# A hybrid scan and attention block on one core: attention, gate and scan interleaved by new costs, and the two maps combined off VectorE

## The chip, the cores and the metric

The kernel runs on one core of a Trainium2 chip. The metric is the device time of one execution in microseconds; the time of the kernel before is the median of three runs.

## The reference, cut to what matters

One layer of a backbone block: 1024 latent and 256 context tokens, width 1024. One input projection feeds two groups. One is a bidirectional Mamba-2 scan (16 heads of 64 in two groups of states, chunks of 128 tokens, forward and backward, with a SiLU gate `z`); the other is differential attention with 4 heads, two softmax maps each. Both outputs are normed, concatenated and projected; a gated MLP follows.

```python
def diff_attention(q, k, v, lam):
    s = jnp.einsum('bqhcd,bkhcd->bhcqk', q.astype(F32), k.astype(F32)) * (DA_QK_DIM ** -0.5)
    p = jax.nn.softmax(s, axis=-1)
    w = p[:, :, 0] - lam * p[:, :, 1]
    return jnp.einsum('bhqk,bkhe->bqhe', w, v.astype(F32))
...
    y_diag = jnp.einsum('bclsgr,bcsgrp->bclgrp', w, xs)
    y_off = jnp.einsum('bclgn,bcgrpn,bclgr->bclgrp', cm, h_starts, jnp.exp(a_cum))
    return y_diag + y_off
...
        yd = _ssd_finish(ssd_chunk_outputs(xs_l, dtl, b_l, c_l, acum_l, hs_l) + dsk * xs_l, rev)
        y_l = yd if y_l is None else y_l + yd
...
    ys_l = rmsnorm(ys_l.astype(pl.dtype) * jax.nn.silu(zl), ssd_norm_g)
```

## The kernel before

`build` runs the stages one after the other: `startup`, `inproj` (all of the input projection but the gate), then the stretch of this change, then `mixffn` (output projection and MLP). In the stretch PE alternates between attention and a filler.

`attention` is a generator over 32 steps n (4 heads x 8 tiles of 128 queries). A step computes two score maps of 128 x 1280 (`scores`, tile `sc`; L814 takes the maximum on VectorE, L815 the exponential on ScalarE into `et`), combines the two maps of the step before in `weigh` (L820 to L823), transposes the result in three pieces on PE (`transpose`, tile `tr`, copied to `wt`) and, for every second step, multiplies with the values (`values`, tile `po`; L851 copies to `oo`, which is stored to `od`). Heads 0 and 1 take 30 value products (split operands), heads 2 and 3 ten. `load_head` loads query tiles S, keys K and values V of a head when its first step comes.

The filler is first `zproj` (384 gate products, tile `pz`, in 16 tiles of 128 x 512; `zo`, the SiLU gate, is stored to `zt`), then `ssd`: states backward (`state`, tiles `xw`, `s`, `hb`), forward (`H0`), and for each of 8 chunks and two groups the function `go` (tiles `scs`, `G`, `yo`, `t`, `y`, `yg`), then `finish` (tile `yt`, gated with `zc` and stored to `yd`).

`run` interleaves them: each `yield` of attention gives a gap in us, times a fill factor; the filler is advanced until the costs that it yields have used up the gap. `self.pin` keeps PE's instructions in the order in which the code issues them; other engines follow the order that a scheduler gives. All loads and stores of the stretch go through SP's queue in the order in which they stand there. What is left of the scan after the last step is run by `ssd_rest` inside `mixffn`, together with the first parts of the attention norm: `o` is loaded from `od` (L1051), squared and summed over columns (`cs_ps`, `cr_ps`), the factor is spread (`dg`, `bc_ps`) and applied (L1062); `yl` is the scan's output loaded back from `yd` (L1072). `pw`, the first output product, follows.

## Time and profile before

| | us |
| --- | --- |
| median of three runs | 1826.5 (1822.24 to 1832.29) |
| the profiled execution | 1826.04 |
| its span | 1824.2 |
| first gate product (`pz`) to first output product (`pw`) | 417.2 to 889.2 |
| PE busy in the span | 1601.6 (88%) |
| VectorE / ScalarE / GpSimd busy | 1222.1 / 753.6 / 1081.2 |

The profile calls TensorE PE, VectorE DVE, ScalarE ACT, GpSimd POOL and the engine that issues the loads SP. A row of a timeline gives the start in us, the duration, the engine, the line, the operation, the tile written and those read, and in brackets how long the engine stood idle ahead of it and what released it. Every matmul but the transposes has the line of a helper, L145, so PE is read by tiles. Records of matmuls overlap, so the price of a packed product is the distance between starts.

### The profile page before, as it was taken

The numbers are of one execution on the slowest core, as the hardware profiler recorded it, in microseconds if no ns is written. First come the engines' busy times: TensorE is split into PE (matmuls) and PEld (weight loads), VectorE is DVE, ScalarE is ACT, GpSimd is POOL, SyncE is SP. The second block draws the span as 40 slices with busy tenths as digits, with TensorE's granted clock in tenths as the row PEclk, the third lists the DMA queues.
The fourth block names the chain that finished last, engine by engine and source line by source line (L and its number), as shares of the span: only waits on it lengthen the run. The fifth ranks groups of instructions, "written<-read, shape, count | busy, mean of one in ns | idle before, by whom it ended". The sixth has DMA issues, their size and how long they took to land.

```text
span 1824.2 us, 21276 instructions
## 1 busy us (share of the span) xinstructions
PE 1601.6 (88%) x7588; PEld 1266.8 (69%) x7588; DVE 1222.1 (67%) x1442; ACT 753.6 (41%) x1395; POOL 1081.2 (59%) x710
## 2 busy tenths in 40 slices
PE   6998998996999888888998958989989998989976
PEld 2797877784778655665677746767777776767755
DVE  4569633352656577877764588766667677898886
ACT  4533676631444333444443443333323334344242
POOL 3322678772100155658566767777778887778741
PEclk8999999998999899999999989999999998999997
DMA  8276767667131667447553312222222225744222
GB/s 310 96 241 218 239 217 246 242 215 224 56 104 46 197 218 213 127 143 234 179 166 114 107 47 98 87 87 93 98 87 87 100 99 187 252 156 127 67 75 93
DMA packets 138826, 273.35 MB, mean 150 GB/s; under 512 B 11984, under 2 KB 60544, under 8 KB 138208
## 3 DMA queue, kind: packets, MB, share of 16 engines
q1 hardware_dynamic: 138128, 271.03, 45.0%
q8 instruction: 60, 0.98, 0.2%
q0 software_dynamic: 592, 0.96, 0.2%
q14 instruction: 46, 0.38, 0.1%
HBM read 197.63 MB, written 74.32 MB: 149 GB/s over the span
## 4 chain that ended last, share of the span: by engine, by line
PE 39%; DVE 18%; POOL 17%; DMA 11%; issue 8%; ACT 6%; SPq 0%; POOLq 0%; DVEq 0%; ACTq 0%
PE pu L145 9%; POOL wlo L126 6%; PE pd L145 6%; POOL S L1205 4%; PE lat L145 4%; PE pz L145 3%; PE pb L145 3%; PE sc L145 3%; DMA K<-kd 3%; PE pw L145 2%; DVE T L126 2%; DMA wt<-wmB 2%; DMA gd<-R 2%; PE po L145 2%; DMA R<-atd 2%
## 5 line engine op out<-in xcount | busy, mean ns | idle before, releaser
L145 PE MATMUL pu<-T,whi 128*128 128x512 f32 x1232 | 387.8, 396 | 8.7 <-ACT whi L125 8.7
L145 PE MATMUL pu<-T,wlo 128*128 128x512 f32 x616 | 248.7, 404 | 44.5 <-POOL wlo L126 36.9
L145 PEld LDWEIGHTS pu<-T,whi 128*128 128x128 f32 x1232 | 235.8, 191 | 58.2 <-ACT whi L125 9.1
L126 POOL TENSOR_TENSOR wlo<-wraw,whi 128x512 fp32r<-128x512 f32 (+2 forms) x118 | 163.4, 1388 | 101.3 <-ACT whi L125 101.2
L145 PE MATMUL lat<-hl,w_hi 128*128 128x512 f32 x640 | 204.6, 396 | 3.0 <-DVE tm L685 2.1
L145 PE MATMUL pd<-T,whi 128*128 128x512 f32 x560 | 183.2, 408 | 15.1 <-ACT whi L125 7.5
L126 POOL TENSOR_TENSOR w_lo<-w_raw,w_hi 128x1024 fp32r<-128x1024 f32 (+1 forms) x36 | 82.7, 2299 | 178.7 <-ACT w_hi L125 156.9
L126 POOL TENSOR_TENSOR wlo<-S,whi 128x512 fp32r<-128x512 f32 (+2 forms) x122 | 171.0, 1411 | 27.6 <-ACT whi L125 27.6
L145 PEld LDWEIGHTS pu<-T,wlo 128*128 128x128 f32 x616 | 117.8, 191 | 86.2 <-POOL wlo L126 49.3
L814 DVE TENSOR_REDUCE stat<-sc 128x1 f32<-128x1280 f32 x64 | 95.2, 1488 | 104.2 <-PE sc L145 104.2
L125 ACT CAST whi<-wraw 128x512 fp32r<-128x512 f32 (+2 forms) x140 | 81.3, 583 | 196.8 <-PE pu L145 108.8
L125 ACT CAST whi<-S 128x512 fp32r<-128x512 f32 (+2 forms) x144 | 81.9, 573 | 150.0 <-PE pu L145 94.7
L145 PEld LDWEIGHTS lat<-hl,w_hi 128*128 128x128 f32 x640 | 121.8, 191 | 28.5 <-DVE tm L685 2.5
L145 PEld LDWEIGHTS pd<-T,whi 128*128 128x128 f32 x560 | 109.5, 197 | 44.2 <-DVE T L126 12.3
L815 ACT ACTIVATE et<-sc,stat 128x1280 f32<-128x1280 f32 x64 | 85.1, 1330 | 130.0 <-DVE stat L814 128.4
L145 PE MATMUL sc<-K,S 128*128 128x512 f32 (+1 forms) x384 | 97.5, 390 | 45.8 <-DMA K<-kd 24.1
L145 PE MATMUL pd<-T,wlo 128*128 128x512 f32 x280 | 115.3, 412 | 15.5 <-POOL wlo L126 15.3
L145 PE MATMUL lat<-hl,w_lo 128*128 128x512 f32 x320 | 126.8, 396 | 0.0
L145 PEld LDWEIGHTS sc<-K,S 128*128 128x128 f32 x384 | 73.5, 200 | 72.8 <-ACT et L815 30.1
L538 POOL TENSOR_TENSOR R<-R,never 128x1024 f32<-128x1024 f32 x32 | 80.6, 2533 | 43.1 <-DMA R<-atd 41.4
L542 ACT ACTIVATE R<-R,lna 128x128 f32<-128x128 f32 x256 | 78.3, 393 | 56.7 <-POOL R L538 56.6
L908 POOL TENSOR_TENSOR xw<-xt,dte 128x1024 f32<-128x1024 f32 x18 | 36.8, 2049 | 93.7 <-DMA xt<-xtok 71.4
(280 smaller groups left out, 3682.0 us busy)
## 6 DMA issues: line engine op xcount, KB each, us to landing
wraw<-wUp SPq DMA_DIRECT2D x46, 512.0 KB, 3.3
wt<-wmB SPq DMA_DIRECT2D x32, 512.0 KB, 4.5
R<-atd SPq DMA_DIRECT2D x32, 512.0 KB, 5.6
stg<-gf_d SPq DMA_DIRECT2D x21, 768.0 KB, 4.8
w_raw<-wU SPq DMA_DIRECT2D x28, 512.0 KB, 5.1
gf_d<-T SPq DMA_DIRECT2D x11, 1024.0 KB, 4.2
K<-kd SPq DMA_DIRECT2D x32, 320.0 KB, 7.8
xt<-xtok SPq DMA_DIRECT2D x19, 512.0 KB, 5.2
```

What stands on the lines that cost most here:

```text
L125: nc.scalar.copy(hi, src)
L126: (lo_eng or nc.vector).tensor_tensor(out=lo, in0=src, in1=hi, op=ALU.subtract)
L145: self.pe(self.nc.tensor.matmul(out, lhsT=lhsT, rhs=rhs, start=start, stop=stop))
L538: nc.gpsimd.tensor_tensor(out=R[:, d], in0=R[:, d], in1=self.never[:, d].unsqueeze(1).broadcast_to([P, 8, P]), op=ALU.add)
L542: nc.scalar.activation(e, e, AF.Exp, bias=self.lna[:, d, i, h:h + 1], scale=1.0)
L814: nc.vector.tensor_reduce(out=st[:, c:c + 1], in_=sc, axis=AX.X, op=ALU.max, negate=True)
L815: nc.scalar.activation(et, sc, AF.Exp, bias=st[:, c:c + 1], accum_out=acc)
L908: nc.gpsimd.tensor_tensor(out=h3(xw), in0=h3(xt), in1=bc_h(self.dte, d, i), op=ALU.mult)
L1205: nc.gpsimd.tensor_tensor(out=t, in0=in0, in1=in1, op=op)
```

## The change

All of it lies between `inproj` and `mixffn`. One balance `self.debt` is carried from the gate products to the scan, with one factor `FILL`; the gaps are new (`FIRST_GAP`, `HEAD_GAP`, `G_ONE`, `G_VAL`, `G_TWO`), and so are the filler's costs. Head 1's keys are loaded into the same pool at step 8 with a gap behind them, and its values at step 10. Head 2 gets a pool of its own, `ap2`, and is loaded when `ssd` starts; head 3 is loaded at step 18. In `weigh` the combination of the maps, one VectorE instruction, becomes a product on ScalarE and a sum on GpSimd. The third transposed piece of heads 2 and 3 is copied by ScalarE.

In the scan the skip term `dsum * x * gate` is computed beside the gate (`zx`, from `xct`, which `inproj` now stores) and added at the end by GpSimd; the chunk's products with `ea` and their sum are made by VectorE straight from PSUM, and `G` is multiplied from PSUM without ScalarE's copy. The state's decay on GpSimd is issued in two halves. `et` has four buffers instead of three, `wt` three instead of four, V one instead of two.

```diff
 F32_FROM = 2
-WT_ENG = "aad"
+WT_ENG = "aaa"
...
-G_B = 2.3
+S_COST = 1.75
+Z_COST = 0.69
+G_ONE = 3.6
+G_VAL = 0.2, 0.2, 1.2, 1.2
+G_TWO = 1.0, 1.0, 0.8
+HEAD_GAP = 4.0
...
 E_W = "ggv"
-FIRST_GAP = 12.0
+FIRST_GAP = 27.0
...
 Y_STEPS = 0, 1, 2, 3, 4, 5, 6, 7, 8, 11, 14
-B_FILL = 1.1
+FILL = 0.98
...
 
-    def run(self, at, filler, fill, drain):
-
-        debt = 0.0
-        for tile_no, gap in at:
-            debt += fill * gap
-            while debt > 0:
+    def run(self, at, filler, drain):
+
+        while True:
+            while self.debt > 0:
                 cost = next(filler, None)
                 if cost is None:
                     if not drain:
                         return
                     break
-                debt -= cost
+                self.debt -= cost
+            gap = next(at, None)
+            if gap is None:
+                return
+            self.debt += FILL * gap
...
-                    if u >= U_B:
+                    if u < U_B:
+                        nc.sync.dma_start(self.xct[u], y[:, CTX:])
+                    else:
                         g = (u - U_B) % 2
                         nc.sync.dma_start((self.bt if u < U_C else self.ct)[g], y[:, CTX:])
...
                              k == 0, k == KT - 1)
                     if k < KT - 1:
-                        yield 0.65
-                zo = zp.tile([P, 512], F32, name="zo")
+                        yield Z_COST
+                xc = zp.tile([P, 512], F32, name="xc", bufs=1)
+                nc.sync.dma_start(xc, self.xct[u][:, sl])
+                zo = zp.tile([P, 512], F32, name="zo", bufs=4)
                 nc.scalar.activation(zo, p, AF.Tanh, scale=0.5)
                 nc.vector.scalar_tensor_tensor(out=zo, in0=zo, scalar=1.0, in1=p, op0=ALU.add, op1=ALU.mult)
                 nc.sync.dma_start(self.zt[u][:, sl], zo)
-                yield 0.65
+                nc.vector.scalar_tensor_tensor(out=xc, in0=xc, scalar=self.dsum[:, u:u + 1], in1=zo,
+                                               op0=ALU.mult, op1=ALU.mult)
+                nc.sync.dma_start(self.zx[u][:, sl], xc)
+                yield Z_COST
...
-            v = []
+            return S, K, []
+
+        def load_values(h, ap):
             for s in range(1 if h >= F32_FROM else 2):
-                vt = ap.tile([P, NT, VD], F32R, name=f"V{s}")
+                vt = ap.tile([P, NT, VD], F32R, name=f"V{s}", bufs=1)
                 nc.sync.dma_start(r32(vt), r32(self.vd[h, s]))
-                v.append(vt)
-            return S, K, v
+                heads[h][2].append(vt)
...
                     self.mm(sc[:, o:o + w], S[c][:, qt * P:(qt + 1) * P], K[c][i][:, o:o + w], i == 0, i == 1)
-            et = ap.tile([P, TOK], F32, name="et", bufs=3)
+            et = ap.tile([P, TOK], F32, name="et", bufs=4)
...
             nc.vector.reciprocal(out=st[:, 5:6], in_=st[:, 4:5])
-            nc.vector.scalar_tensor_tensor(out=st[:, 6:7], in0=st[:, 5:6], scalar=self.nlam[:, 0:1],
-                                           in1=self.s0[:, qt, h:h + 1], op0=ALU.mult, op1=ALU.mult)
-            nc.vector.scalar_tensor_tensor(out=ex[0], in0=ex[1], scalar=st[:, 6:7], in1=ex[0], op0=ALU.mult, op1=ALU.add)
+            nc.vector.tensor_scalar(out=st[:, 6:7], in0=st[:, 5:6], scalar1=self.nlam[:, 0:1],
+                                    scalar2=self.s0[:, qt, h:h + 1], op0=ALU.mult, op1=ALU.mult)
+            nc.scalar.mul(ex[1], ex[1], st[:, 6:7])
+            nc.gpsimd.tensor_tensor(out=ex[0], in0=ex[0], in1=ex[1], op=ALU.add)
...
+        def prefetch(h, pool=ap):
+            heads[h] = load_head(h, pool)
+            if h != 1:
+                load_values(h, pool)
+
+        self.prefetch = prefetch
         n_all = DA_H * NL
         wt, done, prev = None, None, None
         for n in range(n_all + 2):
+            if n in (0, NL, 2 * NL + 2):
+                prefetch({0: 0, NL: 1, 2 * NL + 2: 3}[n])
+                yield {0: FIRST_GAP, NL: HEAD_GAP}.get(n, 0.0)
+            if n == NL + 2:
+                load_values(1, ap)
             if n < n_all:
-                if n % NL == 0:
-                    heads[n // NL] = load_head(n // NL)
-                if n == 0:
-                    yield n, FIRST_GAP
                 st = ap.tile([P, 8], F32, name="stat", bufs=4)
                 e0 = scores(n, 0, st)
             if done is not None:
                 values(*done)
+                yield G_VAL[done[0] // NL]
                 done = None
-                long = False
-            else:
-                long = True
-                yield n, G_LONG if n < n_all else 2.0
+            elif n < n_all:
+                yield G_ONE
             if prev is not None:
                 m, pst, pex = prev
                 w = weigh(m, pst, pex)
             if n < n_all:
                 e1 = scores(n, 1, st)
+            yield G_TWO[0]
             if prev is not None:
                 if m % 2 == 0:
-                    wt = [[ap.tile([P, 4, 256], F32R, name=f"wt{s}", bufs=4) for s in range(2)] for _ in range(3)]
+                    wt = [[ap.tile([P, 4, 256], F32R, name=f"wt{s}", bufs=3) for s in range(2)] for _ in range(3)]
                 for gi in range(2):
                     transpose(m, w, wt, gi)
-                yield n, G_A if long else G_B
+                yield G_TWO[1]
                 transpose(m, w, wt, 2)
                 if m % 2 == 1:
                     done = (m, wt)
-                yield n, G_A if long else G_B
+                yield G_TWO[2]
             prev = (n, st, [e0, e1]) if n < n_all else None
...
     def ssd(self, es):
 
         nc = self.nc
+        self.prefetch(2, self.pool(es, "ap2", 2, side="right"))
         sp = self.pool(es, "sp", 2, side="right")
...
         def state(d, i, prev, xw, bt):
             hn = sp.tile([P, INNER], F32, name="H0" if d == 0 else "hb", bufs=2 if d == 0 else HB_BUFS)
-            if prev is not None:
-                nc.gpsimd.tensor_tensor(out=h3(hn), in0=h3(prev), in1=bc_h(self.cd, d, i), op=ALU.mult)
             for g in range(NG):
                 sl = slice(g * 512, (g + 1) * 512)
+                if prev is not None:
+                    nc.gpsimd.tensor_tensor(out=h3(hn[:, sl]), in0=h3(prev[:, sl]),
+                                            in1=self.cd[:, d, i, 8 * g:8 * g + 8].unsqueeze(2).broadcast_to([P, 8, HD]),
+                                            op=ALU.mult)
                 s = self.pm.tile([P, 512], F32, tag="mm", name="s")
...
             nc.sync.dma_start(zc, self.zt[ks, :, cs].rearrange("k p t -> p k t"))
+            zx = sp.tile([P, 4, P], F32, name="zx", bufs=Z_BUFS)
+            nc.sync.dma_start(zx, self.zx[ks, :, cs].rearrange("k p t -> p k t"))
             G = sp.tile([P, 8, P], F32, name="G", bufs=G_BUFS)
             nc.sync.dma_start(G, self.gd[c, g])
...
             def go():
                 xg = slice(g * 512, (g + 1) * 512)
-                e = [{"p": nc.gpsimd, "d": nc.vector}[x] for x in (ENG_R if self.rest else ENG_B)]
-                if g == 0:
-                    ps = self.pm.tile([P, NG, P], F32, tag="mm", name="scs")
-                    for gg in range(NG):
-                        self.mm(ps[:, gg, :], bl[:, gg, :], cl[:, gg, :])
-                    sc = sp.tile([P, NG, P], F32, name="sc")
-                    nc.scalar.copy(sc, ps)
-                    chunk[c, "s"] = sc
-                    yield M_COST * 0.44
-                nc.vector.tensor_tensor(out=G, in0=G, in1=chunk[c, "s"][:, g, :].unsqueeze(1).broadcast_to([P, 8, P]),
-                                        op=ALU.mult)
-                ts = []
-                for d, st in ((0, self.Hf), (1, hb)):
+                flat = lambda t: t.rearrange("p h d -> p (h d)")
+                ps = self.pm.tile([P, P], F32, tag="mm", name="scs")
+                self.mm(ps, bl[:, g, :], cl[:, g, :])
+                nc.vector.tensor_tensor(out=G, in0=ps.unsqueeze(1).broadcast_to([P, 8, P]), in1=G, op=ALU.mult)
+                yield 0.12
+                t = sp.tile([P, 8, HD], F32, name="t")
+                for d, st in ((1, hb), (0, self.Hf)):
                     po = self.pm.tile([P, 512], F32, tag="mm", name="yo")
                     self.mm(po, cl[:, g, :], st[:, xg])
-                    t = sp.tile([P, 8, HD], F32, name=f"t{d}", bufs=T_BUFS)
-                    if e[d] is nc.gpsimd:
-                        nc.scalar.copy(t.rearrange("p h d -> p (h d)"), po)
-                    src = t if e[d] is nc.gpsimd else h3(po)
-                    e[d].tensor_tensor(out=t, in0=src, in1=self.ea[:, d, i, 8 * g:8 * g + 8].unsqueeze(2)
-                                       .broadcast_to([P, 8, HD]), op=ALU.mult)
-                    ts.append(t)
-                    yield M_COST * 0.85
-                xd = sp.tile([P, 8, HD], F32, name="xd")
-                e[2].tensor_tensor(out=xd, in0=h3(xt[:, xg]), in1=self.dsum[:, 8 * g:8 * g + 8].unsqueeze(2)
-                                   .broadcast_to([P, 8, HD]), op=ALU.mult)
-                e[3].tensor_tensor(out=ts[0], in0=ts[0], in1=ts[1], op=ALU.add)
-                e[4].tensor_tensor(out=ts[0], in0=ts[0], in1=xd, op=ALU.add)
+                    ea = self.ea[:, d, i, 8 * g:8 * g + 8].unsqueeze(2).broadcast_to([P, 8, HD])
+                    nc.vector.tensor_tensor(out=t if d else h3(po), in0=h3(po), in1=ea, op=ALU.mult)
+                    if d == 0:
+                        nc.vector.tensor_tensor(out=flat(t), in0=po, in1=flat(t), op=ALU.add)
+                    yield 0.86
                 y = self.pm.tile([P, 512], F32, tag="mm", name="y")
                 for h in range(8):
                     self.mm(y[:, h * HD:(h + 1) * HD], G[:, h, :], xt[:, (8 * g + h) * HD:(8 * g + h + 1) * HD])
                 yg = sp.tile([P, 512], F32, name="yg")
-                nc.vector.tensor_tensor(out=yg, in0=y, in1=ts[0].rearrange("p h d -> p (h d)"), op=ALU.add)
-                late.append((yg, zc, ks, cs, e[5]))
-                yield M_COST * 0.85
+                nc.vector.tensor_tensor(out=yg, in0=y, in1=flat(t), op=ALU.add)
+                late.append((yg, zc, zx, ks, cs))
+                yield 1.8
                 if len(late) > LAG:
                     yield from finish()
             return go
...
         def finish():
-            yg, zc, ks, cs, e = late.pop(0)
+            yg, zc, zx, ks, cs = late.pop(0)
             pt = self.pm.tile([P, 4, P], F32, tag="mm", name="yt")
             for q in range(4):
                 self.pe(nc.tensor.transpose(pt[:, q, :], yg[:, q * P:(q + 1) * P], self.ident))
-            if e is nc.gpsimd:
-                y = sp.tile([P, 4, P], F32, name="yt")
-                nc.scalar.copy(y, pt)
-            else:
-                y = pt
-            e.tensor_tensor(out=zc, in0=y, in1=zc, op=ALU.mult)
+            nc.vector.tensor_tensor(out=zc, in0=pt, in1=zc, op=ALU.mult)
+            nc.gpsimd.tensor_tensor(out=zc, in0=zc, in1=zx, op=ALU.add)
             nc.sync.dma_start(self.yd[ks, :, cs].rearrange("k p t -> p k t"), zc)
-            yield M_COST * 0.43
+            yield 0.44
```

SP's queue around the first load of the scan's tokens (`xt`), before; S, K and V are head 2's tiles:

```order
L852 DMA od_110<-oo_5175 128x256
L794 DMA K0_5244<-kd_101 64x1280
L789 DMA S_5242<-qd_100 128x1024
L794 DMA K0_5244<-kd_101 64x1280
L794 DMA K1_5247<-kd_101 64x1280 x2
L898 DMA xt_5303<-xtok_102 128x1024
L900 DMA btk_5305<-btok_103 128x256
L898 DMA xt_5309<-xtok_102 128x1024
```

The same place of the change:

```order
L862 DMA od_112<-oo_5009 128x256
L797 DMA S_5091<-qd_100 128x1024
L802 DMA K0_5093<-kd_101 64x1280 x2
L779 DMA zt_106<-zo_5079 128x512
L802 DMA K1_5096<-kd_101 64x1280
L782 DMA zx_108<-xc_5077 128x512
L802 DMA K1_5096<-kd_101 64x1280
L797 DMA S_5099<-qd_100 128x1024
L802 DMA K0_5101<-kd_101 64x1280 x2
L802 DMA K1_5104<-kd_101 64x1280 x2
L811 DMA V0_5107<-vd_99 128x1280
L916 DMA xt_5112<-xtok_102 128x1024
```

In the change `xt` stands behind all of head 2, V included. S_5091 waits for the last gate product, since `ap2` lies where the gate's operands lay.

ACT in a pair of steps that runs beside chunks, before (`et` an exponential, `wt` a copy of transposes, `t0`, `t1` and `yt` copies of the scan):

```order
L851 COPY oo_6036<-po_6025 128x256
L835 COPY wt0_6052<-tr_6058 128x4x128
L835 COPY wt0_6054<-tr_6064 128x4x128
L973 COPY sc_6077<-scs_6074 128x256
L815 ACTIVATE et_6049,stat_6014<-sc_6042,stat_6014 128x1280
L984 COPY t0_6082<-yo_6080 128x512
L984 COPY t1_6091<-yo_6089 128x512
L1013 COPY yt_6114<-yt_6109 128x512
L984 COPY t0_6134<-yo_6132 128x512
L815 ACTIVATE et_6126,s0_95<-sc_6119,stat_6118 128x1280
```

The same engine in such a pair of the change:

```order
L861 COPY oo_6662<-po_6651 128x256
L845 COPY wt0_6690<-tr_6696 128x4x128
L845 COPY wt0_6692<-tr_6702 128x4x128
L824 ACTIVATE et_6687,stat_6640<-sc_6680,stat_6640 128x1280
L845 COPY wt0_6694<-tr_6741 128x2x128
L832 ACTIVATE et_6687<-et_6687,stat_6640 128x1280
L824 ACTIVATE et_6753,s0_95<-sc_6746,stat_6745 128x1280
L845 COPY wt0_6690<-tr_6806 128x4x128
```

The scan's copies are gone. The third copy of `wt` now stands behind the second exponential, and L832, the map's product, behind it.

SP at the end of attention, before:

```order
L1017 DMA yd_109<-zc_6607 128x4x128
L961 DMA zc_6793<-zt_106 128x4x128
L852 DMA od_110<-oo_6816 128x256
L954 DMA bl_7035<-bt_104 128x2x128
L1051 DMA o_6833<-od_110 128x512
L1051 DMA o_6834<-od_110 128x512
```

and in the change, where eight more loads of `yl` stand ahead of these rows:

```order
L1076 DMA yl_7720<-yd_111 128x512
L1076 DMA yl_7742<-yd_111 128x512
L1076 DMA yl_7774<-yd_111 128x512
L862 DMA od_112<-oo_7147 128x256
L1055 DMA o_7164<-od_112 128x512
L1055 DMA o_7165<-od_112 128x512
```

Before, only one small load stood between the last store to `od` and the loads of `o`; `yl` came after them. In the change `yl` comes first.

## Rows read from the trace of the kernel before

**Rows 1.** Stretches: length, busy us of each engine, PE's clock, DMA share, GB/s.

```profile
417.00:460.00 43.00, 25.21 (x92) 19.60 (x91) 15.73 (x16) 8.98 (x13) 10.63 (x6) 0.77 0.80 232
621.00:640.00 19.00, 12.12 (x56) 9.46 (x56) 9.44 (x12) 5.93 (x10) 7.53 (x4) 0.73 1.04 323
640.00:714.00 74.00, 57.55 (x237) 38.98 (x236) 54.73 (x57) 24.91 (x42) 41.71 (x21) 0.95 0.60 199
840.00:890.00 50.00, 41.38 (x193) 23.60 (x193) 43.36 (x65) 24.99 (x52) 34.61 (x25) 0.97 0.48 156
```

**Rows 2.** Timeline of PE: start of attention, and the switch to head 1.

```profile
439.17 0.80 PE L145 MATMUL sc<-K,S 128*128 128x512 f32 x1 [10.28 <-DMA K<-kd]
...
451.20 1.17 PE L145 MATMUL sc<-K,S 128*128 128x512 f32 x5 [1.82 <-DMA K<-kd]
455.40 2.50 PE L145 MATMUL sc<-K,S 128*128 128x512 f32 x6 [3.04 <-ACT et L815]
...
538.62 1.77 PE L145 MATMUL sc<-K,S 128*128 128x512 f32 x5 [2.19 <-DMA K<-kd]
```

**Rows 3.** Timeline of PE in the gate phase, one pair of steps.

```profile
565.22 0.39 PE L145 MATMUL pz<-hl,w_hi 128*128 128x512 f32 x1
565.45 1.32 PE L145 MATMUL sc<-K,S 128*128 128x512 f32 x6
566.61 3.73 PE L145 MATMUL po<-wt,V 128*128 128x256 f32 x30
570.17 1.32 PE L145 MATMUL sc<-K,S 128*128 128x512 f32 x6
...
586.41 1.32 PE L145 MATMUL sc<-K,S 128*128 128x512 f32 x6
```

**Rows 4.** Timelines of PE and POOL at the switch to head 2.

```profile
625.91 0.76 PE L145 MATMUL sc<-K,S 128*128 128x512 f32 x1 [5.16 <-DMA K<-kd]
...
629.81 3.76 POOL L908 TENSOR_TENSOR xw<-xt,dte 128x1024 f32<-128x1024 f32 x2 [71.38 <-DMA xt<-xtok]
```

**Rows 5.** Timeline of PE beside the scan's chunks, one pair of steps.

```profile
742.96 1.41 PE L145 MATMUL sc<-K,S 128*128 128x512 f32 x6
...
761.68 1.42 PE L145 MATMUL sc<-K,S 128*128 128x512 f32 x6 [2.24 <-ACT et L815]
...
768.45 1.41 PE L145 MATMUL sc<-K,S 128*128 128x512 f32 x6
```

**Rows 6.** Timeline of DVE in that pair.

```profile
753.40 2.38 DVE L994 TENSOR_TENSOR t<-t,xd 128x512 f32<-128x512 f32 x1 [0.34 <-POOL t L993]
...
757.29 1.48 DVE L821 SCALAR_TENSOR_TENSOR stat<-stat,nlam,s 128x1 f32<-128x1 f32 x1
758.70 1.48 DVE L814 TENSOR_REDUCE stat<-sc 128x1 f32<-128x1280 f32 x1
760.10 1.54 DVE L823 SCALAR_TENSOR_TENSOR et<-et,stat 128x1280 f32<-128x1280 f32 x1
```

**Rows 7.** Timeline of PE at the last score map.

```profile
814.08 1.43 PE L145 MATMUL sc<-K,S 128*128 128x512 f32 x6 [2.24 <-ACT et L815]
...
830.32 4.48 PE L145 MATMUL po<-wt,V 128*128 128x256 f32 x20
```

**Rows 8.** Groups by line and shape, 410 to 900 us: busy, mean ns, idle before.

```profile
L814 DVE TENSOR_REDUCE stat<-sc 128x1 f32<-128x1280 f32 x64 | 95.2, 1488 | 104.2 <-PE sc L145 104.2
L815 ACT ACTIVATE et<-sc,stat 128x1280 f32<-128x1280 f32 x64 | 85.1, 1330 | 130.0 <-DVE stat L814 128.4
L823 DVE SCALAR_TENSOR_TENSOR et<-et,stat 128x1280 f32<-128x1280 f32 x32 | 61.4, 1918 | 0.6
L993 POOL TENSOR_TENSOR t<-t,t 128x512 f32<-128x512 f32 x16 | 27.7, 1733 | 9.0 <-DVE t L986 7.8 <-DMA o<-od 0.9
L999 DVE TENSOR_TENSOR yg<-y,t 128x512 f32<-128x512 f32 x16 | 10.9, 683 | 0.5
```

**Rows 9.** DMA issues, 410 to 640 and 820 to 940 us: count, KB, median us to landing.

```profile
K<-kd SPq DMA_DIRECT2D x24, 320.0 KB, 8.5
...
o<-od SPq DMA_DIRECT2D x8, 256.0 KB, 5.5
```

24 lines of the change are left out of this document (9 added, 15 removed).

## The prediction

> **What bounds the kernel now.** I read the page's slices first, then a table of stretches, then the timelines of PE, DVE and POOL where the table shows PE idle, and last the grouped instructions for prices. The change touches only the stretch from the last input projection (417.2 us) to the first output product (889.2 us); the other 1352 us run the same code, so the question is how much PE loses in these 472 us. In the table [rows 1] the reader should subtract PE's busy time from each length and add busy time times (1 - clock), since a product at half clock takes twice as long. That gives 17.8 + 5.8 = 23.6 us at the start (417 to 460), 6.9 + 3.3 = 10.2 us at 621 to 640, 16.4 + 2.9 = 19.3 us at 640 to 714 and 8.6 + 1.2 = 9.8 us at 840 to 890. No engine is full in these stretches, so what counts is the waits, each read from a timeline.
>
> At the start PE waits 10.3, 1.8 and 3.0 us for head 0's keys and for the first exponentials [rows 2]; a shorter one for keys lies between. In the gate phase a pair of steps takes 586.41 - 565.45 = 20.96 us [rows 3]. The same rows give packed prices: 0.23 us for one gate product (565.22 to 565.45), 1.16 us for the six products of one score map, 3.56 us for the 30 value products of heads 0 and 1. A pair holds four maps (4.64), the values (3.56), two sets of transposes (about 2.0) and 42 gate products (9.7): 19.9 us, so about 1.1 us is lost in it. At the switch to head 2 PE waits 5.16 us for keys, and POOL starts on the scan only at 629.81 [rows 4]. In the scan a pair of steps takes 25.49 us [rows 5]; by the start-to-start distances of its 18 pieces some 21.4 us are PE's work, so 4 us are lost. The largest wait of the pair, 2.24 us before the map at 761.68, starts on DVE: between 753.40 and 758.70 the next maximum stands behind a sum of 2.38 us and a 128x1 product of 1.48 us [rows 6].
>
> **The change, part by part.** The sum is made against the profiled execution, 1826.04 us (its span 1824.2 us and 1.84 around it); the median shown is 1826.5, so nothing needs shifting.
>
> *Start.* 117 gate products stand ahead of the first map instead of 51: 66 x 0.23 = 15.2 us of work that PE has anyway, laid over the wait for the keys. Head 0's last keys landed at 451.2 [rows 2]; PE reaches the first map at 417.2 + 27.0 = 444.2, the second 4.6 us later (a map and 15 products) at 448.8. Left over are up to 2.4 us for those keys and about 3 us for the first exponential. With the falling clock gone too, 23.6 becomes 5.5 at the best; since the first rounds must still fall into step I take 8.6, a gain of 15 (bounds 10 and 18).
>
> *Gate phase.* 267 products remain behind the first map instead of 333, thus fewer pairs pass beside gate work. Pairs at 1.1 us lost, about six instead of eight: gain 2. Head 1 gets its keys while the filler covers them; the 2.19 us wait at 538.62 [rows 2] goes: gain 2. The added loads of x (16 of 256 KB), stores of zx (16) and 16 SBUF products on DVE cost nothing: PE does not read them, DVE has idle time there. If that cover is gone, one of these products delays a maximum by at most what the wider one at 760.10 takes, 1.54 us [rows 6]; 16 of them at half effect would be 12 us.
>
> *Head 2 and the backward states.* The last gate product now falls near 576 instead of 620. The first order fence shows that SP then issues two S, eight K, V, a zt and a zx before the first xt: 1.05 + 2.62 + 0.66 + 0.52 = 4.85 MB, 5.4 MB with xt itself. At the 323 GB/s of 621 to 640 [rows 1] that is 17 us; with about 3 us of issue and latency (a median K load lands after 8.5 us, [rows 9], most of it in the queue) and 1.9 us for xw (3.76 for two, [rows 4]) the first state product comes 22 us after the last gate product. It stands directly behind it in PE's order, so PE is idle that long and the clock falls as it did before at 621. Before, the same loads started at 608.5 under gate work. Behind it eleven states stand before the first chunk: POOL pays 1.9 for xw and about 1.9 for the decayed state, 9 x 1.9 + 8 x 1.9 = 32 us backward, 6 to 8 forward, and about 3 us for each of four to five map sums: 50 us. PE's work in the same stretch is nine maps (10.4), 60 value products (7.1), transposes (4.0) and states (about 19): 40 us. End 22 + 50 = 72 us after the last gate product, 32 us lost. Before, the time lost from 621 to the first chunk near 714 was 10.2 + 19.3 = 29.5 us [rows 1]. I take +2.5, rounded to 2 (bounds -7, if POOL's sums lie beside waits, and +13, if the loads take 26 us and POOL runs behind).
>
> *Chunks beside attention.* DVE loses the STT of 1918 ns [rows 8] and the SBUF sum of 2.38, and gains products and sums from PSUM; L999, of that kind, takes 683 ns [rows 8]. POOL loses copies' products and three 512-wide sums per group and gains one zx sum per group and the map sum. No row has a 1280-wide POOL sum: from 1.9 us for 1024 columns [rows 4] it would be 2.4 by width, from 1733 ns for 512 columns [rows 8] 4.3. I take 3, nearer the first, whose width is nearer. It lies in the following step, under two maximums and exponentials (1488 and 1330 ns, [rows 8]), so it costs PE nothing, until exponential, product (1.3) and sum together exceed a step of 12 us. The second order fence shows what is new: on ACT the third transpose's copy stands behind the second exponential, so the pair cannot pack fully. I take 24.0 us for a pair (bounds: 22.2, the work and one short wait; 25.5, nothing won). The loss is 2.6 x 7.5 pairs = 19.5 us against 4.1 x 5 pairs = 20.5 before: 0 in all, since all eight chunks are now inside attention.
>
> On the sum put on POOL, the rows first: the SBUF sum L994 took 2.38 us at 753.40 where POOL ran beside it, and L999, whose input is in PSUM, 683 ns. The Trainium skill (Perfetto Trace Analysis, Optimizing Scalar/DVE Operations) warns that moving work between VectorE and GpSimd might not help as they share a port; SBUF — State Buffer, "SBUF: two separate sides", limits this to VectorE operations with two SBUF inputs or in a two-port mode. The trace agrees with the second, and what DVE keeps in the scan reads PSUM. Taken the other way it is a rival, below.
>
> *Tail.* Before, the last map began at 814.08, the last values at 830.32 [rows 7]; three whole chunks then filled PE while o was loaded and normed. Now everything hangs on one chain behind the last map: maximum, exponential, product, sum (1.5 + 1.5 + 1.3 + 3), transposes and copies (2.5), 20 value products (4.3), copy and store (2.9), load of o (5.5, [rows 9]) = 22.5 us. From o's landing (836.1 + 5.5 = 841.6) to the first output product at 889.2 47.6 us went by before, 31 of them work of three chunks (21.4 less maps, values and transposes, 10.4 each): the norm alone takes between 17 us and all 47, and I take 25, nearer the first, as PE lost only 9.8 us from 840 on [rows 1]. So 47.5 us pass, with 19 of PE work (the transposes of outputs and of the last two steps, 3; the values, 4; the norm's sums and spreads, 12): 28.5 lost. Before, the 73.8 us from the end of the last map (815.4) held some 52 of work by start-to-start distances, 22 lost: +7 (bounds 0 and +18).
>
> Sum: -15 - 2 - 2 + 2 + 0 + 7 = -10, and 1826 - 10 = **1816 us**.
>
> **The rivals.** *Pairs bound by PE (faster):* with DVE's 1918 ns and 2.38 us pieces gone, a pair takes 22.2 us; 7.5 x 1.8 = 13.5 us less, 1802. For it: PE is the fullest engine in the first three stretches of the table. Against: ACT's new order.
> *Slower:* the scan's inputs stand behind head 2's loads. If they land 27 us after the last gate product instead of 20 and POOL then needs 58 us for eleven states and five sums at the upper price, the backward stretch loses 45 to 47 us instead of 32: +14; that alone is 1830. The third fence has the same thing at the end: eleven loads of the scan's output ahead of the last od store and of o, through three buffers; two rounds of them at o's 5.5 us would be 11 more, 1841. Slower than before begins where the two together exceed 10 us, so where the backward stretch ends later than 82 us after the last gate product. For it: the order on SP. Against: POOL was busy for only 41.7 of the 74 us from 640 to 714 [rows 1].
> *POOL's sum blocks DVE:* if DVE waits for half of each 3 us sum, two in a pair, 7.5 pairs lose 3 us each, and the time is 1838. [rows 6] show sums from SBUF stretched, [rows 8] L999 not, so it gets 5 in 100.
> *The waits only move:* PE's stall at the start goes to the head 2 switch, and the chunks that no longer cover the norm cost what the start wins, 15 us for 15: about 1826.
>
> **How the numbers follow.** My forecast (1805 to 1826, centre 1816) gets 0.40, PE-bound pairs 0.20, the slower one 0.18 and POOL's blocking 0.05, no net change 0.17. The independent bounds, 4 us at the start, 10 for the states, 12 for the pairs and 9 for the tail, come to 18 us in root-sum-square. About 1.4 times that on either side takes in the rivals: the range of 8 in 10 is 1790 to 1842; the forecast alone, 1805 to 1826. Half a per cent, 9 us, is about what a measurement can tell. Faster than 1817: the PE-bound case and two thirds of the forecast, 0.47; slower than 1836: 0.22; the same 0.31.
>
> **What would show it.** The first map at about 444 with waits of under 6 us to 460; a gap on PE of 20 to 26 us right behind the last gate product near 576, with POOL's first xw at its end; pairs of about 24 us with the maximum directly behind its map; the last map near 832; L833 on POOL at 2.4 to 4.3 us; 45 to 50 us from the last map to the first output product near 880. The prediction is wrong if that gap is short (faster), if pairs stay at 25.5 us, or if the last od store waits long behind the output loads (slower).

## The result and the profile after

The changed kernel took 1845.25 us in the median of five runs (1842.54 to 1846.89); its ratio to the kernel before is 1.0095, 95% interval 1.0071 to 1.0119. It is slower by 0.95%, outside the forecast's range and on the other side. The profiled execution has a span of 1845.1 us.

First the page's line of busy times, then a table of the same stretches as in [rows 1] (length, busy us of each engine, PE's clock, DMA share, GB/s), cut at the changed kernel's own places: start, gate phase, the gap behind the last gate product, states, chunks, tail.

```profile
PE 1602.9 (87%) x7588; PEld 1264.6 (69%) x7588; DVE 1183.9 (64%) x1456; ACT 770.5 (42%) x1389; POOL 1089.7 (59%) x700
```

```profile
406.00:460.00 54.00, 39.95 (x163) 32.15 (x161) 18.89 (x22) 12.54 (x17) 15.10 (x8) 0.82 0.74 219
460.00:588.00 128.00, 117.26 (x638) 97.83 (x636) 74.60 (x99) 69.56 (x106) 38.55 (x15) 0.97 0.38 117
588.00:612.00 24.00, 0.28 (x2) 0.26 (x2) 3.34 (x3) 2.02 (x3) 5.04 (x3) 0.55 0.98 275
612.00:669.00 57.00, 47.00 (x192) 29.76 (x193) 32.62 (x49) 21.28 (x32) 46.52 (x32) 0.89 0.87 282
669.00:857.00 188.00, 171.11 (x942) 132.84 (x941) 129.67 (x173) 86.23 (x130) 89.77 (x51) 0.98 0.62 189
857.00:915.00 58.00, 31.90 (x100) 15.33 (x99) 32.02 (x57) 39.41 (x75) 22.36 (x15) 0.76 0.42 134
```

PE's work is the same as before (1602.9 against 1601.6 us), and DVE's is 38 us less: the change took work off DVE and gained nothing by it. With the forecast's formula (length less busy, plus busy times 1 - clock) PE loses 21.2 us at the start, 14.3 in the gate phase, 23.8 in the gap, 15.2 in the states, 20.3 in the chunks and 33.8 in the tail: 128.6 in all. The rows of the kernel before that [rows 1] lack, cut at the same places (gate phase, chunks up to the last map, tail), are these:

```profile
460.00:621.00 161.00, 153.03 (x854) 129.78 (x852) 102.97 (x133) 76.43 (x130) 10.61 (x4) 0.99 0.27 78
715.00:814.00 99.00, 87.49 (x467) 66.83 (x465) 81.51 (x80) 45.46 (x79) 65.70 (x47) 0.98 0.54 163
814.00:889.00 75.00, 64.78 (x316) 41.30 (x317) 61.13 (x81) 33.48 (x69) 54.23 (x37) 0.95 0.51 163
```

With [rows 1] that is 23.6 us at the start, 9.5 in the gate phase, 29.5 in gap and states, 13.3 in the chunks and 13.5 in the tail, 89.4 in all. Of the 39 us that came on top, the tail has 20.3, gap and states 9.5 (39.0 now), the chunks 7.0 and the gate phase 4.8; the start won 2.4.

The places, from first to last, against the forecast:

| | forecast | measured |
| --- | --- | --- |
| first gate product | 417.2 | 406.9 |
| from there to the first map | 27.0 | 26.5 |
| from the first gate product to the last | 159 | 180.7 |
| from it to the first chunk | 72 | 81.4 |
| first chunk to last map | 184 | 186.9 |
| last map to first output product (`pw`) | 47.5 | 58.6 |
| from there to the end of the span | 935.0 | 930.6 |

The differences, 21.7 + 9.4 + 2.9 + 11.1 - 10.3 - 4.4 = 30.4, are, up to rounding, the 31 us between the forecast span (1814) and the measured one. The next rows show where the first three come from: PE's timeline at the start and behind the last gate product, then DVE's and SP's at the start, then POOL's in the states.

```profile
433.41 1.32 PE L142 MATMUL sc<-K,S 128*128 128x512 f32 x6
449.03 2.50 PE L142 MATMUL sc<-K,S 128*128 128x512 f32 x6 [10.87 <-ACT et L824]
...
611.74 2.08 PE L142 MATMUL s<-xw,btk 128*128 128x512 f32 x2 [23.72 <-POOL xw L926]
```

```profile
445.33 0.75 DVE L780 SCALAR_TENSOR_TENSOR xc<-xc,c_dskp,zo 128x512 f32<-128x512 f32 x1 [15.16 <-DMA xc<-xct]
446.00 1.48 DVE L823 TENSOR_REDUCE stat<-sc 128x1 f32<-128x1280 f32 x1
...
463.51 2.83 DVE L780 SCALAR_TENSOR_TENSOR xc<-xc,c_dskp,zo 128x512 f32<-128x512 f32 x1 [0.46 <-DMA xc<-xct]
```

```profile
420.61 2.74 SPq L802 DMA_DIRECT2D K<-kd  x4
...
424.03 4.57 SPq L802 DMA_DIRECT2D K<-kd  x4
...
432.79 0.32 SPq L775 DMA_DIRECT2D xc<-xct  x1
```

```profile
637.08 2.92 POOL L833 TENSOR_TENSOR et<-et 128x1280 f32<-128x1280 f32 x1
639.96 1.90 POOL L926 TENSOR_TENSOR xw<-xt,dte 128x1024 f32<-128x1024 f32 x1
641.82 1.04 POOL L934 TENSOR_TENSOR hb<-hb,cd 128x512 f32<-128x512 f32 x1
```

The first map no longer waits for its keys [rows 2]: it starts at 433.41 without a wait. But its maximum starts only at 446.00, 11 us after the map is done. DVE stood idle for 15.16 us ahead of it, on the new zx product L780, whose x tile was issued on SP at 432.79, behind head 0's keys. PE's wait for keys (10.28 before) has become a wait of 10.87 for the first exponential.

In the tail, the chain that ended last (start, us, what):

```profile
863.07 2.90 DMA yl<-yd
...
870.48 2.76 DMA yl<-yd
...
875.67 2.71 DMA yl<-yd
...
879.03 0.27 ACT oo L861
...
879.39 3.06 DMA od<-oo
```

The loads of the scan's output pass one after the other ahead of the last copy of o, as the forecast's slower rival had it. ScalarE works on them too, and the last copy of o (L861) comes behind that work.

Three prices came out as forecast: the POOL sum (L833) takes 2931 ns in the mean, the decay's two halves 1042 ns each, and DVE's products from PSUM 681 to 690 ns. The rows of the sum, of the zx product and of one product from PSUM:

```profile
L833 POOL TENSOR_TENSOR et<-et 128x1280 f32<-128x1280 f32 x32 | 93.8, 2931 | 131.1 <-ACT et L832 108.3 <-issue 16.6 <-DMA xc<-xct 5.5
L780 DVE SCALAR_TENSOR_TENSOR xc<-xc,c_dskp,zo 128x512 f32<-128x512 f32 x16 | 19.7, 1230 | 27.5 <-DMA xc<-xct 27.2
L999 DVE TENSOR_TENSOR yo<-yo,acum 128x512 f32<-128x512 f32 x16 | 11.0, 690 | 11.7 <-PE yo L142 11.7
```

### The profile page after: what moved, and what is told of

It is laid out like the page before. It is cut to its first block, busy times and chain, and to the rows that moved or that the text cites. A ratio compares the mean times of both kernels' runs of the same rounds, so it can differ in the third digit from the quotient of the medians.

```text
span 1845.1 us, 21460 instructions
## 1 busy us (share of the span) xinstructions
PE 1602.9 (87%) x7588; PEld 1264.6 (69%) x7588; DVE 1183.9 (64%) x1456; ACT 770.5 (42%) x1389; POOL 1089.7 (59%) x700
## 3 DMA queue, kind: packets, MB, share of 16 engines
q1 hardware_dynamic: 152336, 287.80, 47.5%
## 4 chain that ended last, share of the span: by engine, by line
PE 40%; POOL 18%; DVE 14%; DMA 11%; issue 11%; ACT 6%; SPq 0%; DVEq 0%; POOLq 0%; ACTq 0%
PE pu L142 8%; POOL wlo L123 7%; PE pd L142 6%; POOL S L1209 4%; PE lat L142 4%; PE sc L142 3%; PE pb L142 3%; PE po L142 3%; PE pw L142 2%; DVE T L123 2%; PE pz L142 2%; DMA wt<-wmB 2%; DMA xc<-xct 1%; POOL R L539 1%; POOL u L1263 1%
## 5 line engine op out<-in xcount | busy, mean ns | idle before, releaser
L142 PE MATMUL pd<-T,whi 128*128 128x512 f32 x560 | 180.7, 403 | 15.9 <-DVE T L123 9.1
L833 POOL TENSOR_TENSOR et<-et 128x1280 f32<-128x1280 f32 x32 | 93.8, 2931 | 131.1 <-ACT et L832 108.3
L122 ACT CAST whi<-S 128x512 fp32r<-128x512 f32 (+2 forms) x144 | 81.7, 572 | 148.8 <-PE pu L142 90.6
L823 DVE TENSOR_REDUCE stat<-sc 128x1 f32<-128x1280 f32 x64 | 95.3, 1489 | 53.7 <-PE sc L142 53.6
```

The costliest lines, as they stand in the source:

```text
L122: nc.scalar.copy(hi, src)
L142: self.pe(self.nc.tensor.matmul(out, lhsT=lhsT, rhs=rhs, start=start, stop=stop))
L823: nc.vector.tensor_reduce(out=st[:, c:c + 1], in_=sc, axis=AX.X, op=ALU.max, negate=True)
L833: nc.gpsimd.tensor_tensor(out=ex[0], in0=ex[0], in1=ex[1], op=ALU.add)
```

## The experiments

Eighteen kernels ran beside the kernel before. A ratio is the time over that of the kernel before, run beside it, with its 95% interval; stretches are from each kernel's own timeline. The changed kernel's own ratio is 1.0095 (1.0071 to 1.0119).

### The start

**e1_xc3.**

```diff
-                xc = zp.tile([P, 512], F32, name="xc", bufs=1)
+                xc = zp.tile([P, 512], F32, name="xc", bufs=3)
```

> The changed kernel with three buffers instead of one for xc, so that its loads can be issued ahead of head 0's keys. Theory A (the changed kernel lost most at the start because DVE's zx products wait for xc and the maximums stand behind them): the wait of 10.9 us before the map at 449 goes or falls below 4 us, the clock holds at the start, and the kernel comes to 1830 to 1836 us, 10 to 15 less than 1845. Theory B (the loss is the longer way of the maps over ACT and POOL): the maximums stay as late, at most 4 us are won.

Ratio 1.0081 (1.0050 to 1.0111). The first maximum still waits, now for the fourth tile's x (16.40 us, DVE at 446.46), and PE 12.1 us for the first exponential: by the terms set down, the run speaks for Theory B, and only i3 below shows that Theory A had the place right. From the first to the last gate product 172.0 us go by instead of 180.7. That gain lies behind the start: PE's waits for late `wt` from 460 us to the last gate product, in the changed kernel and then here (total, times, longest):

```profile
PE tr L841 <- DVE wt L123: 10.7, 7, 3.1
```

```profile
PE tr L841 <- DVE wt L123: 4.3, 7, 1.6
```

The kernel before waits 3.8 us there; f5_fill and j2 below, with one buffer for xc, wait 10.8 and 11.2. The first chunk now waits 13.0 us for its reload of hb instead of 4.1, so most of what was won came back.

**f1_xc5.** The same with five buffers for xc, and two instead of four for `zo`.

> The changed kernel with five buffers for xc (and two instead of four for zo), so that the loads of all five gate tiles ahead of the first map stand ahead of head 0's keys; with three the fourth load still stood behind them, and the first maximum waited for it as long as before (12.1 us). Theory A (DVE's first maximum waits behind a zx product whose xc is in the queue behind the keys): the wait of 11 to 12 us before the map at 449 falls to about 3, the last gate product comes 8 to 12 us earlier than with three buffers, counted from the first. Theory B (the first maximum waits for something else): no change at that place. In the total: 8 to 12 us less than the changed kernel if nothing is given back later; no more than 5 if the time comes back at the scan's loads, as it did with three buffers (a wait of 13 us for the first hb).

Ratio 1.0141 (1.0116 to 1.0166). The wait stays (11.4 us), with a new cause: ACT's gate waits for a `zo` buffer whose store stands behind the keys.

```profile
450.77 0.60 ACT L777 ACTIVATE zo<-pz 128x512 f32<-128x512 f32 x1 [14.55 <-DMA zt<-zo]
```

A store of the gate now does what a load did before: it needs the queue while the keys pass through, and the first maximum comes at 452.79, behind it.

**h4_gap12.**

```diff
-FIRST_GAP = 27.0
+FIRST_GAP = 12.0
```

> The changed kernel with the old first gap of 12 (51 gate products ahead of the first map instead of 117), nothing else changed. Theory A (the gate tiles ahead of the first map bring their zx products and stores into the queue behind the keys, and these hold up the first maximum): the first map waits 8 to 12 us for its keys as before, but the maximum follows it at once; in all 3 us less to 5 us more. Theory V (the early gate products are a gain that is lost elsewhere): 10 us or more slower than 1845.

Ratio 1.0098 (1.0066 to 1.0130), the changed kernel's own. The wait for keys is back (10.8 us at most), the one for the first exponential down to 2.3. By the formula PE loses 23.0 us up to 460 us, against 21.2 in the changed kernel: at the start the 66 products moved ahead win 2 us, where the forecast had put 15. The equal total is no clean test of them, since the filler that starts later also ends later: the tail loses 25.2 us instead of 33.8, gap and states 57.2 instead of 39.0.

### Head 2, the tokens and head 3

**e3_xt.** Manual order on SP: head 2's loads, now called inside the scan, behind the first two loads of the scan's tokens.

```diff
+            if h == 2:
+                self.tc.add_manual_dep(ld.ins, self.tok_ld.ins.name, ...
```

> The changed kernel with head 2's loads kept behind the first two loads of the scan's tokens. Theory A (PE's gap of 23.7 us is the scan's tokens standing behind 4.9 MB): the gap falls below 8 us, and 10 to 18 us are won, 1827 to 1835. Theory B (POOL bounds the states, the loads only set when it starts): the gap falls, but the waits come back at the states; less than 6 us are won. A third case: head 2's keys come too late for their first map, whose step waits; then nothing is won.

Ratio 1.0146 (1.0112 to 1.0180). The gap falls from 24.1 to 10.3 us, and the third state waits 12.89 us for its tokens, which now come behind head 2; PE then waits 12.9 us for the first hb. From the last gate product to the first chunk 79.9 instead of 81.4 us, and the chunks take 194.8 instead of 186.9. Nothing is won.

```profile
599.29 5.85 PE L142 MATMUL s<-xw,btk 128*128 128x512 f32 x8 [9.89 <-POOL xw L931]
...
620.06 1.22 PE L142 MATMUL s<-xw,btk 128*128 128x512 f32 x1 [12.89 <-POOL xw L931]
```

**g1_noap2.** Heads 2 and 3 loaded at steps 16 and 24 into the shared buffers, no `ap2`.

```diff
-        self.prefetch(2, self.pool(es, "ap2", 2, side="right"))
...
-            if n in (0, NL, 2 * NL + 2):
-                prefetch({0: 0, NL: 1, 2 * NL + 2: 3}[n])
+            if n in (0, NL, 2 * NL, 3 * NL):
+                prefetch(n // NL)
```

> The changed kernel without a pool of its own for head 2: heads 2 and 3 are loaded at their first steps into the buffers of the heads before, all else as changed. Theory C (what the early end of the gate wins is lost because head 2, the scan's tokens, the states' stores and head 3 all pass the DMA queue in 80 us): the gap behind the last gate product falls from 24 to 6 to 12 us, a wait of 5 to 12 us for head 2's keys comes instead; from the last gate product to the first chunk 70 to 76 us instead of 81; total 1835 to 1841. Theory D (POOL's 50 us of states and sums bound that stretch): 78 us or more remain, the total within 4 us of 1845.

Ratio 1.0144 (1.0109 to 1.0178). The gap falls to 5.6 us and the first chunk comes 68.8 us after the last gate product, better than theory C said; but maps wait 4.7 us and, beside the chunks, 8.9 us for keys, the chunks take 195.1 us instead of 186.9 and the tail 66.0 instead of 58.6. The pool of its own is not what makes the change slow.

**f2_h3.** Head 3 loaded at step 22 instead of 18, its loads on SP behind the first reloads of hb.

```diff
-            if n in (0, NL, 2 * NL + 2):
+            if n in (0, NL, 2 * NL + 6):
...
+            if h == 3:
+                self.tc.add_manual_dep(ld.ins, self.hb_ld.ins.name, ...
```

> The changed kernel with head 3 loaded four steps later and kept behind the first reload of hb in SP's queue. Theory C: the wait for hb at the first chunk (4.1 us) goes and the loads of the states flow sooner: 4 to 8 us less than 1845. Theory D: at most 3 us.

Ratio 1.0085 (1.0058 to 1.0112), an interval that overlaps the changed kernel's. In the profile the wait for hb is gone and the chunks take 181.5 us instead of 186.9; by itself that is not clear of noise in the time.

### The sum of the maps

**e4_stt.** The one DVE instruction in place of L832 and L833.

> The changed kernel with the two maps combined on DVE by one instruction again, all else as changed. Theory A: the sum on POOL costs little; without it the chunks lose 0 to 8 us (a DVE instruction of 1.5 to 1.9 us a step), the tail wins 3; within 6 us of 1845. Theory B (the way over ACT and POOL is the loss): 15 us or more are won, 1830 or less.

Ratio 1.0163 (1.0134 to 1.0193). Undoing this part costs about 12 us: beside the chunks DVE's instruction takes 1750 ns in the mean, the chunk's `G` comes later (PE waits 9.2 us for it instead of 3.9), the chunks take 193.7 us. Theory B falls; Theory A had the chunks right but missed the total, as 4.8 us more go by up to the last gate product (185.5 us) as well.

The run also bears on the states. From the last gate product to the first chunk, first in the changed kernel and then here:

```profile
588.00:669.00 81.00, 47.27 (x193) 30.02 (x193) 35.96 (x52) 23.29 (x35) 51.56 (x34) 0.79 0.90 280
```

```profile
592.00:674.00 82.00, 47.48 (x196) 29.73 (x194) 42.31 (x56) 18.52 (x32) 44.27 (x30) 0.81 0.89 280
```

Without the map sums POOL is busy for 7 us less, and the stretch is as long (81.7 us against 81.4).

**e5_comb.** This part alone on the kernel before.

> The kernel before with only the combination of the maps moved from DVE (one instruction of 1918 ns) to a product on ACT and a sum on POOL. Theory A (good by itself: undoing it in the changed kernel cost 12 us): 5 to 12 us faster than before, 1814 to 1821. Theory B (POOL carries 30 of 40 us in that kernel's chunks and the sum comes behind three sums of the scan): 5 us or more slower.

Ratio 1.0001 (0.9981 to 1.0021): neither theory, but no change. There POOL still has the scan's sums, and the sum of the maps takes 3184 ns beside the chunks. By these two runs the part is worth something only together with the rest.

### The tail

**e2_yl.** Manual order on SP: loads of `yl` behind those of `o`.

> The changed kernel with the loads of the scan's output kept behind the loads of o in SP's queue. Theory A (od's last store and o wait behind eleven output loads, which wait for buffers): from the last map to the first output product 47 to 50 us instead of 58.6, in all 8 to 11 us less, 1834 to 1837. Theory B (the norm's own chain is that long): at most 3 us less.

Ratio 1.0121 (1.0089 to 1.0154). From the last map to the first output product 62.6 us instead of 58.6: Theory A is wrong. With o first, the work on `yl` falls into the norm, and PE waits for DVE's `dg` there (8.5 us). The chain through the `yl` loads was what ended last, and what stands next is as long.

**f5_fill** and **j2.** The scan's balance alone (j2 with 0.7).

```diff
-            self.debt += FILL * gap
+            self.debt += (0.8 if drain else FILL) * gap
```

> The changed kernel with the balance of the scan at 0.8 instead of 0.98 of each gap, so that about two and a half chunks are left when attention ends and run beside the attention norm, as three did before; nothing else changed. Theory T (the tail is where the gain went: 58.6 us from the last map to the first output product with 32 us of PE work): PE's loss in the tail falls from 34 us to 12 to 18, the pairs of steps shorten by the work that leaves them, total 1828 to 1835. Theory U (the pairs are bound by their own waits, not by PE's work, and keep 22.5 to 25 us with less work in them): within 5 us of 1845.

> The changed kernel with the scan's balance at 0.7, nothing else changed. If the uncovered tail is the larger part of the loss: 1822 to 1830, the same as before within its interval. If 0.8 had covered it already: 1833 to 1838.

Ratios 1.0053 (1.0032 to 1.0073) and 1.0006 (0.9982 to 1.0030). f5_fill falls just short of its Theory T: 1836.3 us in the median, with 20.5 us lost in the tail (840 to 902). With one number changed, j2 is back at the time of before. Its last three stretches, states, chunks and tail:

```profile
615.00:689.00 74.00, 57.34 (x259) 39.09 (x260) 39.69 (x58) 29.68 (x45) 56.83 (x37) 0.89 0.88 272
689.00:833.00 144.00, 131.65 (x715) 102.59 (x714) 95.08 (x126) 78.36 (x118) 70.86 (x38) 1.00 0.54 174
833.00:893.00 60.00, 53.74 (x258) 34.43 (x257) 42.05 (x78) 23.37 (x47) 15.45 (x12) 0.94 0.54 167
```

The tail is about as long as in the changed kernel (60.3 us against 58.6), but holds 53.7 us of work instead of 31.9: PE loses 9.5 us there instead of 33.8, and attention ends sooner by the chunks that left it. The chunks lose 12.4 us instead of 20.3; the states lose 23.0 instead of 15.2, so part of the gain is given back there. The rest of the span, behind the first output product, differs as well, though its code is the same: 924.5 us here, 930.6 in the changed kernel, 935.2 in j1 below; that is not explained.

### Together

**h2_fill, i2, j1.** Three buffers for xc, head 3 as in f2_h3, and a balance of 0.8, 0.7 and 0.6.

> The changed kernel with three buffers for xc, head 3 loaded four steps later and behind the first reload of hb, and the scan's balance at 0.8. If the three places add up (start 4, head 3 6, tail 12): 1820 to 1826, no slower than before. If what is won at one is lost at the next, 1832 or more.

> h2_fill with the balance at 0.7 instead of 0.8, so that about three and a half chunks are left for the tail. If the tail is still uncovered: 3 to 6 us less than 1814. If it is covered by two and a half chunks: within 3 us, or slower.

> i2 (three buffers for xc, head 3 behind the first hb) with the balance at 0.6 instead of 0.7. If chunks left over keep covering the tail: 1798 to 1804. If beyond three and a half the rest of the scan runs alone behind the norm and PE waits there: 1806 or more.

Ratios 0.9931 (0.9907 to 0.9956), 0.9905 (0.9868 to 0.9942) and 0.9976 (0.9953 to 1.0000). The parts more than add up: e1_xc3, f2_h3 and f5_fill are 0.0014, 0.0010 and 0.0042 below the changed kernel's ratio, h2_fill 0.0164 (1814.0 us in the median, where 1820 to 1826 was expected). Why they win more together is not shown. i2, 1805.2 us in the median, beats both kernels. Tails of i2 and j1:

```profile
817.00:878.00 61.00, 54.79 (x261) 34.85 (x260) 42.79 (x79) 23.56 (x48) 15.94 (x12) 0.94 0.53 164
```

```profile
807.00:884.00 77.00, 66.40 (x318) 41.68 (x317) 53.91 (x96) 24.67 (x50) 21.14 (x16) 0.93 0.56 176
```

At 0.6 what is left of the scan outlasts the norm: the last chunk's products end only where the output projection begins, 76.8 us after the last map instead of 60.6 in i2.

**i1, i3, i4.** On h2_fill: head 2 behind two token loads (i1), the zx product as two products on POOL (i3), and both (i4).

> h2_fill (three buffers for xc, head 3 behind the first reload of hb, balance 0.8) and head 2's loads behind the first two loads of the scan's tokens. If the gap of 24 us behind the last gate product is a loss of its own: it falls to about 10 and 8 to 14 us are won against h2_fill, 1800 to 1806. If only the DMA queue counts, which head 2, tokens and states fill either way: the time comes back as waits for tokens, within 4 us of 1814.

> h2_fill with the zx product made by two products on POOL instead of one on DVE. Theory A (the first maximum waits on DVE behind the zx product whose xc comes late): PE's wait of 11.7 us before the second map after the start falls below 4 us, and the last gate product comes 8 us or more earlier, counted from the first; 1804 to 1809 in all. Theory B (the wait has another cause, the stores or the keys): it stays.

> i1 and i3 together. If both win and add up: 1792 to 1800. If the second gives back the first: no better than the better of the two.

Ratios 0.9952 (0.9930 to 0.9974), 0.9971 (0.9955 to 0.9986) and 0.9983 (0.9966 to 1.0001): none beats h2_fill. In i1 the gap falls to 10.9 us and the first chunk still comes 86.8 us after the last gate product (84.8 in h2_fill), as e3_xt showed on the other base. In i3 the wait of the first maximum is gone. PE's waits from the first gate product to 460 us, first of h2_fill, then of i3 (total, times, longest):

```profile
PE sc L142 <- ACT et L829: 13.4, 2, 11.7
```

```profile
PE sc L142 <- DMA K<-kd: 2.4, 1, 2.4
PE sc L142 <- ACT et L829: 1.8, 1, 1.8
```

From the first to the last gate product i3 takes 166.7 us instead of 172.0, 5.3 less where 8 were expected. That the zx product on DVE holds up the first maximum is thereby shown. The total does not show it, since i3's first gate product comes 7.9 us later. The code ahead of it is the same; why it takes longer is not shown.

### The input projection

**e6_xct.** The kernel before, with x's tiles stored for nobody to read.

```diff
-                    if u >= U_B:
+                    if u < U_B:
+                        nc.sync.dma_start(self.xct[u], y[:, CTX:])
+                    else:
```

> The kernel before with nothing changed but that the input projection also stores x's eight tiles (xct), which nothing reads. The changed kernel's first gate product came 10 us earlier than that of before. Theory E (the stores change the order that the scheduler gives the input projection, and that order is 10 us faster): first gate product at 406 to 411, total 1816 to 1820. Theory F (the 10 us come from other instructions' order, drawn by what follows): 415 to 418, total 1824 to 1830.

Ratio 0.9952 (0.9928 to 0.9976), 8.5 us less by the medians; first gate product at 409.5. Theory E holds for this pair of kernels. With the same store in their input projection, though, the other kernels have their first gate product anywhere from 406.0 (f2_h3) to 414.3 us (i3), so the store alone does not set it. PE's waits for the copies of transposed tokens (`st`) ahead of the gate (total, times, longest), before and in e6_xct:

```profile
PE ptr L619 <- ACT st L620: 13.3, 8, 5.7
```

```profile
PE ptr L620 <- DVE st L621: 5.8, 2, 4.3
```

## Why the prediction was wrong, step by step

Two steps failed above all: the side work that was to "cost nothing" at the start and in the gate phase, and the +7 for the tail. By the busy rows the start won 2.4 us instead of 15, the gate phase lost 4.8 instead of winning 4, and the tail lost 20.3 more instead of 7.

*Start: "The added loads of x ... cost nothing".* This step failed, and with it the gain of 15. PE does not read these tiles, but DVE works in order, and the scores' first maximum stands behind them. At the start their loads and stores pass the queue with head 0's keys. I priced the products by their duration (at most 1.54 us, from one row, though [rows 8] have that instruction at 1918 ns in the mean) and not by what they wait for: 15.16 us. h4_gap12 shows that the early gate products win 2 us at the start, i3 shows the wait's cause. In the gate phase head 1's wait for keys went, as forecast, but PE lost 10.7 us on late `wt` (3.8 before). Three buffers for xc bring that down to 4.3 (e1_xc3), so the loads of x through one buffer cost the gate phase about 6 us. The zx product also stretches to 2.83 us where POOL works beside it; with three buffers it still does (2.41 us), so the stretching is the smaller part.

*Gap and states.* The 22 us forecast for the gap were 24.1, and POOL's prices were right; the states took 57.3 us instead of 50. The step that failed is that POOL's work sets their length. POOL was busy for 46.5 of the 57 us, but without the map sums the stretch is as long (e4_stt), and g1_noap2 passes it in 68.8 us with POOL busy for 55.7. e3_xt and i1 move the wait from the first state to the third, with 0.87 of the DMA's time taken: head 2, tokens, states' stores and head 3 pass the queue in 80 us, whichever is first. Shown by them is that the order of head 2 and tokens doesn't matter; that the volume alone sets the 81 us is only argued. An estimate from the rows, rate times length, fits it: 23 MB in the 81 us (280 GB/s), 20 MB in the 69 us of g1_noap2 (292 GB/s).

*Chunks.* 24.0 us were forecast for a pair; the seven pairs took 22.0 to 25.2, 23.4 in the mean (value products from 686.16 to 849.91), with the wait for the third transposes that the order showed (5.5 us in all). The stretch took 186.9 us against 184: right. What failed is its result, "0 in all, since all eight chunks are now inside attention". I counted this as neutral and only charged the norm's longer chain with 7.

*Tail.* Here the place was right and the size wrong: 58.6 us from the last map instead of 47.5. The chain up to o was put at 22.5 us and the norm at 25; the first use of o came 28.6 us after the last map, and from there to the first output product it took 30.0.

```profile
884.51 0.61 ACT L179 ACTIVATE sq<-o 128x512 f32<-128x512 f32 x1
```

The loss before was sized too high as well: 22 us by distances from start to start, where the row of 814 to 889 gives 13.5. So 33.8 us lost are 20.3 more, not 7. The rival with the output loads ahead of o named the chain, but e2_yl shows that their order alone isn't the cause. The cause is that no scan work is left: j2 gives chunks back to the tail and the ratio falls from 1.0095 to 1.0006, some 16 us, with nothing else changed. The balance (`FILL` of 0.98 with the new gaps and costs) was the dearest choice in the diff, and I had not priced it as a choice.

*The map sum.* Its price and its being hidden were right, and e4_stt shows that it helps where DVE carries the chunks. The rival in which POOL's sum blocks DVE does not show in the chunks: L999, L1001 and L1007 keep 681 to 690 ns. It shows in L780 and, in the tail beside other POOL work, in L1079 (739 to 1818 ns); both have two inputs in SBUF. The Trainium skill (SBUF — State Buffer, "SBUF: two separate sides") says that VectorE contends with GpSimd for their shared ports only with two SBUF inputs or in a two-port mode. These rows agree with it.

*Not forecast.* The first gate product came 10.3 us earlier. e6_xct gets 7.7 of that from a store that nobody reads. That was luck, and an estimate from the two figures is that without it the change would have been some 8 to 10 us slower still.

What stays open: what sets the 81 us from the last gate product to the first chunk, what sets the end of the input projection, and why the three parts win more together than apart.

## What to carry to other kernels

A filler that hides one phase is missing in the next: before filler is moved into one phase, count what PE has to do behind the last step, where the chain is serial. An instruction put "beside" the path costs what it waits for, if it stands on an in-order engine ahead of the path's next step; look where its input comes from and what shares the queue at that moment. And when a gap goes, look at the next wait on the same queue before counting the gain.

## What the runs showed of the hardware that was not expected

A 512-wide DVE product with two inputs in SBUF (L780) takes 0.75 us alone and up to 2.66 and 2.83 beside a POOL instruction, while products from PSUM (L999, L1001, L1007) stay at 0.68 to 0.69. PE's granted clock came to 0.55 in the 24 us gap, with 0.28 us of work in it, and to 0.76 in the mean of the tail. There the 20 value products took 6.16 us (870.60) instead of 4.48 (849.91). So an uncovered stretch is paid twice: once in idle time and once in its own products, part of them at the lower level (1.2 of 2.4 GHz).
